# A recurrence among fill products: scores moved to chunks 0 and 1, more products a group, DVE's order written by hand

## The chip, the cores and the metric

One core of one Trainium2 chip runs the whole program. The metric is device microseconds for one execution. Engines are named as in the profile: PE (TensorE matmul), PEld (its weight loads), DVE (VectorE), ACT (ScalarE), POOL (GpSimd), SP (SyncE, which issues the DMAs here).

## The reference, cut to what matters

Two layers over 272 tokens (16 meta tokens and 256 real ones) of width 2048, all in float32: an RWKV-7 time mix, a squared-ReLU MLP, a gated linear attention, a second MLP, and a last norm. Only the time mix is touched by the change. Its core is a scan over tokens, for each of 32 heads of width 64:

```python
def step(S, inp):
    r_t, w_t, k_t, v_t, a_t, b_t = inp
    sa = einsum('bhvk,bhk->bhv', S, a_t)
    S = S * w_t[:, :, None, :] + sa[..., None] * b_t[:, :, None, :] + v_t[..., None] * k_t[:, :, None, :]
    y = einsum('bhvk,bhk->bhv', S, r_t)
    return S, y
```

Ahead of it stand the projections r, k and v and the low-rank decay and rate; behind it a per-head norm, a bonus term, a gate, and the output matrix `w_o`.

## The kernel before, in words

**Products.** Float32 matrices are multiplied in three passes. A weight piece of 128 x 1024 is loaded (`wload`, L122), ACT rounds it to `hi` (L132), DVE forms `lo = raw - hi` (L133), each in two halves in this stage, and PE adds hi·xh, hi·xl and lo·xh (`mm3`, L136; profile lines L138 to L140). One such triple of matmuls of 272 columns is called a *product* here; a piece holds eight. There are three `raw` buffers and two of `hi` and `lo`.

**The recurrence in chunks.** The scan is done in chunks of 64 tokens: four full ones and one of 16. Heads are taken in four groups g of eight. Within a chunk the scan is a triangular system. `scores` (L403) forms its matrices, eight matmuls a chunk, masked by two DVE operations. `invert` (L419) inverts all triangular blocks of a group at once on DVE: ten transposes into `sysA`, thirty elimination steps (each an `upd` product and a subtraction from `sysA`, the second needing the first), twelve transposes back. It is a generator with 52 steps, so that it can be spread over other work. `merge` (L518) joins 32 x 32 blocks to 64 x 64 on PE in two halves (profile lines L530 and L540), with ACT copies between.

**A chunk's chain.** `state` (L579) multiplies the state S into the chunk's rows and DVE forms `rs`; `solve` (L593) applies the inverse; `emit` (L604) makes the new S on PE (L611), which DVE adds and scales (two operations), and the outputs (L619); `inner` (L569) prepares the next chunk's `rs`. `turn` (L624) transposes outputs back to `hres`; `centre` (L548) and `keys` (L561) prepare values and keys. `norm(g)` (L635) is a generator of eight steps for the group's head norm and gate, with PE matmuls L643 and L652.

**Fill.** PE is kept busy beside this chain by 448 products: the v projection (256), `outA` (128) and half of `outB` (64). `R(n)` runs the next n of them and `until(n)` runs up to the n-th. The v projection of a column ends with an ACT copy and a DVE add to `rr`.

**What sets the order.** PE's order in this stage is the program's (`manual_schedule`, L745). All other engines, DVE among them, are ordered by the compiler's scheduler from priorities. `wload` has a high priority. The table `GAPS` (L46) gives for each group and chunk how many products stand between `state` and `solve`, and between `solve` and `emit`. After the last chunk `until(V - 8)` runs 120, 184 or 248 products in all, the rest of the inversion is issued, and `merge` follows. In group g, the scores of the next group are placed in chunks 0, 1 and 2, and `invert` starts in chunk 2, with 6 and 8 steps ahead of `solve` and of `emit`.

**The key stage ahead.** For each of 16 columns f: two weight pieces of `w_k`, exponentials on ACT, some sixteen DVE operations, and stores of `bk` and `ar` to DRAM, from which `load` (L398) brings a group back. Inversion 0 is issued whole at f = 13, its scores at f = 9.

Of the kernel before, what the change touches and what calls it, by code (L numbers as in the profile page):

```python
# [17 lines left out]
P = 128  # L18
# [9 lines left out]
NG = 4  # L28
# [14 lines left out]

GAPS = [[(2, 1), (2, 1), (2, 1), (8, 8), (8, 8)],  # L46
# [3 lines left out]


class Kern:
# [211 lines left out]
    def rwkv(self, done):  # L264
# [133 lines left out]
        def load(g, bk=True, ar=True):  # L398
            for on, dst, src in ((bk, BKs, bkd), (ar, ARs, ard)):
                if on:  # L400
                    nc.sync.dma_start(dst[g % 2], src[4 * g : 4 * g + 4].rearrange("f p n -> p f n"))

        def scores(g, c):  # L403
            BK, AR, AM, AMr = (b[g % 2] for b in (BKs, ARs, AMs, AMrs))
# [43 lines left out]
        for f in range(KT):  # L448
            r = rr[f]
            bk, ar = st2[0][f % 2], st2[1][f % 2]  # L450
            ps = self.proj(pair(wk, f), xk, T, bank=self.ptr if f % 2 else None)
            ca = self.t(ep, [P, 2, T], "ca", 2)
            nc.sync.dma_start(ca.rearrange("p a t -> p (a t)"), cad[f])
            iW, kk, sq, kn = (self.t(ep, [P, T], n, 2) for n in ("iW", "kk", "sq", "kn"))
            nc.scalar.activation(W, ca[:, 0], AF.Exp, scale=-DECAY)
            nc.scalar.activation(iW, ca[:, 0], AF.Exp, scale=DECAY)
            nc.scalar.mul(kk, ps, self.vec("k_k", f))
            nc.scalar.activation(sq, kk, AF.Square)
            nc.scalar.activation(kn, ca[:, 1], AF.Identity, scale=self.vec("k_a", f), bias=self.omka[:, f : f + 1])
# [12 lines left out]
            nc.vector.scalar_tensor_tensor(out=kn, in0=r, scalar=self.vec("r_k", f), in1=kn, op0=ALU.mult, op1=ALU.mult)  # L472
            put(ar, 1, r, W)
            nc.sync.dma_start(ard[f], ar)
            rk = self.pm()[:, :T]
            nc.tensor.matmul(rk, self.bones, kn, start=True, stop=True)
            nc.scalar.copy(r, rk)
            nc.vector.tensor_copy(WC[:, f], W[:, C - 1 : 4 * C : C])
            if f == 3:
                xv = mix(3, self.xp)  # L480
                early2.close()
                wl = ExitStack()
                lp = wl.enter_context(tc.tile_pool(name="wl", bufs=1, reuse_waits="tile"))
                BKs, ARs = ([self.t(lp, [P, 4, 576], n)] for n in ("BK0", "AR0"))
                AMs, AMrs = [self.t(lp, [P, NC4, 8, 128], "AM0")], [self.t(lp, [64, 8, 64], "AMr0")]
                sysA = self.t(lp, [P, 32, 32], "sysA")
                t11 = sysA.rearrange("p a b -> p (a b)")[64:96].rearrange("p (c h s) -> p c h s", c=NC4, h=8)
                nc.gpsimd.memset(sysA, 0.0)
            if f == 7:
                load(0)  # L490
            if f == 9:
                for c in range(5):
                    scores(0, c)
            if f == 13:
                for _ in invert(0):
                    pass
        early.close()

        win = ExitStack()
# [165 lines left out]
        loc = [hres[:, f] if f < 12 else rr[f - 4] for f in range(KT)]  # L665


        def units(x, srcs, ps):
            for i, s in enumerate(srcs):
                hi, lo = self.wload(s)  # L670
                for j in range(8):
                    kt = 8 * i + j
                    self.mm3(ps, hi, lo, slice(j * P, (j + 1) * P), x[kt][:, 0], x[kt][:, 1], kt == 0,
                             kt == 8 * len(srcs) - 1)
                    if kt < 8 * len(srcs) - 1:
                        yield

        def v_proj(f):
            ps = self.pj()[:, :T]
            yield from units(xv, pair(wv, f), ps)  # L680
            nc.scalar.copy(hres[:, f], ps)
            tt(rr[f], rr[f], hres[:, f])
            yield

        def outA(f):
            ps = self.pj()[:, :T]
            yield from units(yo, [ap["rw_oA"][f]], ps)
            xin = rr[f % 8] if f < 12 else loc[f]
            nc.sync.dma_start(xin, ap["hT"][:, f])
            tt(loc[f], ps, xin, ALU.add)  # L690
            yield

        def outB(s, fp):
            hi, lo = self.wload(ap["rw_oB"][s, fp])
            pss = [self.pj()[:, :T] for _ in range(2)]
            for i in range(2):
                for j in range(4):
                    y = yo[8 + 4 * s + j]
                    self.mm3(pss[i], hi, lo, slice((4 * i + j) * P, (4 * i + j + 1) * P), y[:, 0], y[:, 1], j == 0, j == 3)
                    if j < 3:  # L700
                        yield
                f = 2 * fp + i
                tt(hres[:, f] if s else loc[f], pss[i], loc[f], ALU.add)
                if s:
                    done(f)
                yield

        def products():
            for f in range(KT):
                yield from v_proj(f)  # L710
            split(0)
            split(1)
            for f in range(8):
                yield from outA(f)
            split(2)
            for f in range(2):
                yield from outB(0, f)
            for f in range(8, 12):
                yield from outA(f)
            for f in range(2, 6):  # L720
                yield from outB(0, f)
            for f in range(12, 16):
                yield from outA(f)
            for f in range(6, 8):
                yield from outB(0, f)

        work = products()
        ran = [0]
# [13 lines left out]
        nothing = iter(())  # L742
        self.split_parts = 2
        load(1)
        with tc.manual_schedule(engines={mybir.EngineType.PE}):  # L745
            until(52)
            m = merge(0)
            next(m)
# [4 lines left out]
                f(0, 0)  # L753
            inv = last = nothing
            for g in range(NG):
                V = 64 * (g + 2) if g < 3 else 0
                for c in range(5):
                    if c:
                        state(g, c)
                        turn(g, c - 1)  # L760
                    if g + 1 < NG and c in (1, 2):
                        scores(g + 1, 2 * c - 1)
                        R(1)
                    else:
                        some(last, 1)
                        R(GAPS[g][c][0])
                    some(inv, 6)
                    solve(g, c)
# [12 lines left out]
                    if c < 4:  # L781
                        inner(g, c + 1)
                    if c == 2 and g + 2 < NG:
                        load(g + 2, ar=False)
                some(last, 99)
                if g + 2 < NG:
                    load(g + 2, bk=False)
                if g + 1 < NG:
                    until(V - 8)
                    some(inv, 99)  # L790
                    m = merge(g + 1)
                    next(m)
                    until(V)
                    turn(g, 4)
                    R(4)
                    next(m)
                    for f in (centre, keys, inner):
                        f(g + 1, 0)
                    R(3)
                else:  # L800
                    turn(g, 4)
                last = norm(g)
        for _ in last:
            R(4)
        R(999)
        win.close()
        wl.close()
        split(3)
        for f in range(8):
            for _ in outB(1, f):  # L810
                pass
        self.split_parts = 1
        outer.close()

# [249 lines left out]
```

## Time and profile before

| what | us |
|---|---|
| median of 3 runs | 2668.19 (2666.27 to 2672.52) |
| the profiled execution | 2671.53 |
| its span | 2669.7 |
| PE, DVE, ACT busy | 2553.1, 1687.8, 1258.0 |
| PE waiting for an inversion's end, 318 to 700 us | 47.9 |

The first 300 us or so are the projections r and k; the recurrence lies between about 320 and 680; the rest are `outB`, the MLPs and the attention. A busy PE in this profile is not PE at its peak: matmuls are pipelined, so that a product is priced by the time from start to start. PEclk is the clock that the throttle granted, 1.00 at best.

### The profile page before, as it was taken

The page shows a single profiled execution, that of the slowest core. Times are in us where ns is not written, and L with a number is a line of the kernel's source. Part 1 is how long each engine was busy: PE and PEld are TensorE (multiplying, and loading weights), DVE is VectorE, ACT ScalarE, POOL GpSimd, SP SyncE. Part 2 cuts the span into 40 slices and gives each one's busy share as a digit, 9 for nine tenths or more (in the row PEclk, how much of TensorE's full clock was granted, in tenths as well). Part 3 has the DMA queues.
Part 4 walks back from the last instruction along what each step waited for, and adds up shares of the span by engine and source line. Part 5 has one row for each costly group of instructions (what it writes and reads, how often), then busy time and mean ns, then how long its engine had stood idle before and what let it go on. Part 6 is the DMA issues. An engine that isn't in the chain of part 4 may idle for free.

```text
span 2669.7 us, 47686 instructions
## 1 busy us (share of the span) xinstructions
PE 2553.1 (96%) x19492; PEld 2369.1 (89%) x19492; DVE 1687.8 (63%) x2794; ACT 1258.0 (47%) x2011; POOL 10.8 (0%) x35
## 2 busy tenths in 40 slices
PE   7999887779999999999999999999999999999998
PEld 7888886668999999999999999988888888888887
DVE  8678966674755545545545666776766656656665
ACT  5465543435554434434434544454555535435444
POOL 0000000000000000000000000000000000000000
PEclk9999988889999999999999999999999999999999
DMA  5567622213445555545555544444555555555554
GB/s 189 177 226 260 223 92 72 85 58 106 160 166 177 179 174 175 179 176 174 176 179 174 178 152 144 174 150 142 190 184 188 189 190 189 188 187 188 188 189 158
DMA packets 136026, 450.16 MB, mean 169 GB/s; under 512 B 14704, under 2 KB 22640, under 8 KB 135808
## 3 DMA queue, kind: packets, MB, share of 16 engines
q1 hardware_dynamic: 135808, 447.12, 48.4%
q8 instruction: 153, 2.51, 0.4%
q14 instruction: 65, 0.53, 0.1%
HBM read 431.07 MB, written 15.99 MB: 167 GB/s over the span
## 4 chain that ended last, share of the span: by engine, by line
PE 76%; DVE 1%; ACT 0%; issue 0%; DVEq 0%
PE pj L166 23%; PE pj L138 13%; PE pj L140 13%; PE pj L139 13%; PE pj L167 12%; PE pt L899 1%; DVE lo L133 0%; PE pu L908 0%; PE pm L652 0%; PE pt L888 0%; PE pu L910 0%; PE pu L909 0%; PE pm L845 0%; PE pm L643 0%; DVE hres L978 0%; DVE sg L927 0%
## 5 line engine op out<-in xcount | busy, mean ns | idle before, releaser
L133 DVE TENSOR_TENSOR lo<-raw,hi 128x1024 fp32r<-128x1024 f32 (+1 forms) x834 | 946.8, 1142 | 617.4 <-ACT hi L132 603.9
L132 ACT CAST hi<-raw 128x1024 fp32r<-128x1024 f32 (+1 forms) x834 | 813.4, 983 | 1098.5 <-PE pj L139 585.3
L138 PE MATMUL pj<-x,hi 128*128 128x272 f32 x2224 | 661.7, 298 | 6.6 <-ACT x L306 4.1
L140 PE MATMUL pj<-x,lo 128*128 128x272 f32 x2224 | 649.2, 292 | 0.0
L139 PE MATMUL pj<-x,hi 128*128 128x272 f32 x2224 | 647.3, 291 | 0.0
L166 PE MATMUL pj<-x,hi 128*128 128x512 f32 x1664 | 587.9, 397 | 0.6 <-DVE x L818 0.6
L167 PE MATMUL pj<-x,lo 128*128 128x256 f32 x1664 | 469.5, 282 | 1.3 <-DVE lo L133 1.3
L138 PEld LDWEIGHTS pj<-x,hi 128*128 128x128 f32 x2224 | 425.6, 191 | 15.3 <-ACT x L306 4.9
L139 PEld LDWEIGHTS pj<-x,hi 128*128 128x128 f32 x2224 | 428.1, 192 | 2.1
L140 PEld LDWEIGHTS pj<-x,lo 128*128 128x128 f32 x2224 | 424.9, 191 | 0.7
L166 PEld LDWEIGHTS pj<-x,hi 128*128 128x128 f32 x1664 | 313.5, 188 | 76.2 <-issue 2.9
L166 PE MATMUL pj<-h,hi 128*128 128x512 f32 x1024 | 358.5, 395 | 0.0
L167 PEld LDWEIGHTS pj<-x,lo 128*128 128x128 f32 x1664 | 315.0, 189 | 2.9 <-DVE lo L133 1.9
L138 PE MATMUL pj<-h,hi 128*128 128x272 f32 x1024 | 295.3, 288 | 0.0
L140 PE MATMUL pj<-h,lo 128*128 128x272 f32 x1024 | 294.4, 288 | 0.0
L139 PE MATMUL pj<-h,hi 128*128 128x272 f32 x1024 | 294.0, 287 | 0.0
L167 PE MATMUL pj<-h,lo 128*128 128x256 f32 x1024 | 288.9, 282 | 0.0
L166 PEld LDWEIGHTS pj<-h,hi 128*128 128x128 f32 x1024 | 192.7, 188 | 43.6
L167 PEld LDWEIGHTS pj<-h,lo 128*128 128x128 f32 x1024 | 194.3, 190 | 0.0
L139 PEld LDWEIGHTS pj<-h,hi 128*128 128x128 f32 x1024 | 194.1, 190 | 0.0
L138 PEld LDWEIGHTS pj<-h,hi 128*128 128x128 f32 x1024 | 193.2, 189 | 0.0
L140 PEld LDWEIGHTS pj<-h,lo 128*128 128x128 f32 x1024 | 192.4, 188 | 0.0
(246 smaller groups left out, 2213.9 us busy)
## 6 DMA issues: line engine op xcount, KB each, us to landing
raw<-mlp_w_d SPq DMA_DIRECT2D x512, 512.0 KB, 3.2
raw<-gla_in_d SPq DMA_DIRECT2D x98, 512.0 KB, 3.2
raw<-w_rkv_d SPq DMA_DIRECT2D x80, 512.0 KB, 3.4
raw<-gla_o_d SPq DMA_DIRECT2D x32, 512.0 KB, 3.2
raw<-w_r_d SPq DMA_DIRECT2D x16, 512.0 KB, 3.3
raw<-rw_oA_d SPq DMA_DIRECT2D x16, 512.0 KB, 3.2
raw<-rw_oB_d SPq DMA_DIRECT2D x16, 512.0 KB, 3.2
ard<-ar SPq DMA_DIRECT2D x16, 288.0 KB, 3.5
```

What stands on the lines that cost most here:

```text
L132: nc.scalar.copy(hi[:, h], raw[:, h])
L133: nc.vector.tensor_tensor(out=lo[:, h], in0=raw[:, h], in1=hi[:, h].bitcast(F32), op=ALU.subtract)
L138: nc.tensor.matmul(out, hi[:, ws], xh, start=first, stop=False)
L139: nc.tensor.matmul(out, hi[:, ws], xl, start=False, stop=False)
L140: nc.tensor.matmul(out, lo[:, ws], xh, start=False, stop=last)
L166: nc.tensor.matmul(wide, hi[:, ws], x[kt][:, :, off : off + SEQ], start=kt == 0, stop=False)
L167: nc.tensor.matmul(ps[:, :SEQ], lo[:, ws], x[kt][:, 0, off : off + SEQ], start=False, stop=kt == nk - 1)
L899: nc.tensor.matmul(pa[:w, i * C : (i + 1) * C], KX[i][:, dt, s * P : s * P + w], Q[:, dt, i * C : (i + 1) * C], start=dt == 0, stop=dt == 1)
```

## The change

It has five parts, all in the RWKV-7 function.

1. Scores of the next group go to chunks 0 and 1 alone (0 and 1 in chunk 0; 2, 3 and 4 in chunk 1). `invert` starts at the end of chunk 1, with nine steps ahead of each `solve` and each `emit`.
2. `GAPS` has 8 or 9 products twice in chunks 2 to 4 of groups 0 to 2, and 4 twice in all chunks of group 3. The merge comes after product 134, 214 or 286 (`MARK`); ahead of it in a group run 72 to 80 products from the last merge.
3. Inversion 0 is spread over the key products: seven steps a column from f = 8, after loads at f = 4 and scores at f = 6.
4. Weight pieces come from one list, and `ahead()` issues the load and the split of the next piece at the fourth product of the present one.
5. `manual_schedule` holds for DVE too, so its order there is the program's. The loads for group g + 2 are issued in chunks 2, 3 and 4, the second array cut at column 512.

```diff
-GAPS = [[(2, 1), (2, 1), (2, 1), (8, 8), (8, 8)],
-        [(2, 1), (2, 1), (2, 1), (8, 8), (8, 8)],
-        [(2, 1), (2, 1), (2, 2), (10, 10), (10, 10)],
-        [(2, 2), (2, 2), (10, 10), (10, 10), (10, 10)]]
+GAPS = [[(2, 1), (2, 1), (8, 8), (9, 9), (9, 9)],
+        [(2, 1), (2, 1), (8, 8), (9, 9), (9, 9)],
+        [(2, 1), (2, 1), (8, 8), (8, 8), (8, 8)],
+        [(4, 4), (4, 4), (4, 4), (4, 4), (4, 4)]]
+MARK = [134, 214, 286]
...
-            if f == 7:
+            if f == 4:
                 load(0)
-            if f == 9:
+            if f == 6:
                 for c in range(5):
                     scores(0, c)
-            if f == 13:
-                for _ in invert(0):
-                    pass
+                inv = invert(0)
+            if f > 7:
+                for _ in range(7):
+                    next(inv, None)
...
-        def units(x, srcs, ps):
-            for i, s in enumerate(srcs):
-                hi, lo = self.wload(s)
+        def units(x, n, ps):
+            for i in range(n):
+                hi, lo = weights.pop(0)
                 for j in range(8):
+                    if j == 3:
+                        ahead()
...
+        def ahead():
+            if srcs:
+                weights.append(self.wload(srcs.pop(0)))
...
+        ahead()
-        with tc.manual_schedule(engines={mybir.EngineType.PE}):
+        with tc.manual_schedule(engines={mybir.EngineType.PE, mybir.EngineType.DVE}):
...
-                    if g + 1 < NG and c in (1, 2):
-                        scores(g + 1, 2 * c - 1)
-                        R(1)
-                    else:
+                    if more and c < 2:
+                        scores(g + 1, 2 * c)
+                    elif not more:
                         some(last, 1)
-                        R(GAPS[g][c][0])
-                    some(inv, 6)
+                    R(GAPS[g][c][0])
+                    some(inv, 9)
                     solve(g, c)
...
-                    if g + 1 < NG and c < 3:
-                        scores(g + 1, 2 * c)
-                        if c == 2:
-                            inv = invert(g + 1)
-                    some(last, 3)
+                    if more and c < 2:
+                        scores(g + 1, 2 * c + 1)
+                    some(last, 4)
                     R(GAPS[g][c][1])
-                    some(inv, 8)
+                    if more and c == 1:
+                        scores(g + 1, 4)
+                        inv = invert(g + 1)
+                    some(inv, 9)
                     emit(g, c)
...
-                    until(V - 8)
+                    until(MARK[g])
                     some(inv, 99)
                     m = merge(g + 1)
                     next(m)
-                    until(V)
+                    R(4)
                     turn(g, 4)
-                    R(4)
+                    R(2)
                     next(m)
                     for f in (centre, keys, inner):
                         f(g + 1, 0)
-                    R(3)
+                    R(4)
```

The order of all other instructions in the stage, and what is computed, stay as they were.

More of the change, by code (lines that the diff above doesn't have):

```diff
@@ L396, in put, with fetch, load @@
             tt(dst[:, o + skip : o + 16], a[:, 4 * C + skip :], b[:, 4 * C + skip :])
[L398 to L401, printed above, removed]
+        def fetch(g, dst, src, a=0, b=576):
+            nc.sync.dma_start(dst[g % 2][:, :, a:b], src[4 * g : 4 * g + 4, :, a:b].rearrange("f p n -> p f n"))
+        def load(g):
+            fetch(g, BKs, bkd)
+            fetch(g, ARs, ard)
         def scores(g, c):
@@ L679, in v_proj @@
             ps = self.pj()[:, :T]
-            yield from units(xv, pair(wv, f), ps)
+            yield from units(xv, 2, ps)
             nc.scalar.copy(hres[:, f], ps)
@@ L686, in outA @@
             ps = self.pj()[:, :T]
-            yield from units(yo, [ap["rw_oA"][f]], ps)
+            yield from units(yo, 1, ps)
             xin = rr[f % 8] if f < 12 else loc[f]
@@ L697, in outB @@
                 for j in range(4):
+                    if (i, j) == (0, 3):
+                        ahead()
                     y = yo[8 + 4 * s + j]
@@ L706, in outB @@
                 yield
-        def products():
[L709 to L725, printed above, removed]
+        order = [(v_proj, f) for f in range(KT)] + [(split, 0), (split, 1)] + [(outA, f) for f in range(8)] + [(split, 2)]
+        order += [(outB, 0, 0), (outB, 0, 1)] + [(outA, f) for f in range(8, 12)] + [(outB, 0, f) for f in range(2, 6)]
+        order += [(outA, f) for f in range(12, 16)] + [(outB, 0, 6), (outB, 0, 7), (split, 3)]
+        order += [(outB, 1, f) for f in range(8)]
+        srcs = []
+        for k, *a in order:
+            srcs += pair(wv, a[0]) if k == v_proj else [ap["rw_oA"][a[0]]] if k == outA else [ap["rw_oB"][a[0], a[1]]] if k == outB else []
+        weights = []
+        def ahead():
+            if srcs:
+                weights.append(self.wload(srcs.pop(0)))
+        def products():
+            for k, *a in order:
+                if k == split:
+                    split(*a)
+                else:
+                    yield from k(*a)
         work = products()
@@ L744, in rwkv @@
         load(1)
-        with tc.manual_schedule(engines={mybir.EngineType.PE}):
+        ahead()
+        with tc.manual_schedule(engines={mybir.EngineType.PE, mybir.EngineType.DVE}):
             until(52)
@@ L755, in rwkv @@
             for g in range(NG):
-                V = 64 * (g + 2) if g < 3 else 0
+                more = g + 1 < NG
                 for c in range(5):
@@ L782, in rwkv @@
                         inner(g, c + 1)
[L783 to L788, printed above, removed]
-                    until(V - 8)
+                    if g + 2 < NG and c == 2:
+                        fetch(g + 2, BKs, bkd)
+                    if g + 2 < NG and c == 3:
+                        fetch(g + 2, ARs, ard, 0, 512)
+                    if g + 2 < NG and c == 4:
+                        fetch(g + 2, ARs, ard, 512)
+                if more:
+                    until(MARK[g])
                     some(inv, 99)
@@ L804, in rwkv @@
             R(4)
-        R(999)
+        until(448)
         win.close()
         wl.close()
[L808 to L811, printed above, removed]
+        R(999)
         self.split_parts = 1
```

7 lines of the change are left out of this document (3 added, 4 removed).

## The prediction

> **What bounds the kernel now.** I read the page first (span), then a table of busy time by stretches, cut at events of the recurrence, then the waits, then the order of time.
>
> ```profile
> span 2669.7 us, 47686 instructions
> ```
>
> ```profile
> 328.16:350.39 22.23, 20.50 (x286) 18.47 (x287) 5.50 (x10) 9.61 (x22) 0.94 (x1) 0.70 0.26 94
> 350.39:410.67 60.28, 44.98 (x670) 40.80 (x666) 51.01 (x121) 20.91 (x48) 0.68 (x2) 0.88 0.30 102
> 410.67:435.23 24.56, 22.28 (x322) 19.65 (x323) 8.28 (x16) 13.01 (x31) 0.94 (x1) 0.88 0.18 62
> 435.23:448.58 13.35, 11.21 (x176) 8.99 (x173) 6.38 (x13) 6.25 (x15) 0.52 (x1) 1.00 0.12 32
> 448.58:459.90 11.32, 8.37 (x158) 6.99 (x159) 9.26 (x19) 2.93 (x8) 0.00 (x0) 1.00 0.38 130
> 459.90:473.15 13.25, 12.30 (x168) 11.34 (x169) 12.35 (x34) 5.36 (x12) 0.16 (x1) 0.87 0.21 73
> 473.15:499.26 26.11, 12.76 (x158) 11.91 (x159) 24.71 (x61) 7.01 (x15) 0.00 (x0) 0.79 0.38 131
> 499.26:589.91 90.65, 66.97 (x976) 59.03 (x977) 63.22 (x149) 36.93 (x88) 1.62 (x3) 0.88 0.18 60
> 589.91:678.15 88.24, 83.53 (x1077) 75.77 (x1078) 43.52 (x88) 47.04 (x106) 0.52 (x1) 0.96 0.29 97
> 678.15:743.61 65.46, 62.97 (x490) 61.53 (x488) 51.74 (x105) 35.96 (x72) 0.00 (x0) 1.00 0.46 162
> ```
>
> Columns: stretch, length, busy PE, PEld, DVE, ACT, POOL, granted clock, DMA share, GB/s. The cuts are the first matmul of a merge (328.16, 410.67, 499.26, 589.91) or of a `state` (350.39, 435.23, 448.58, 459.90, 473.15); 678.15 is the last norm's end, 743.61 the MLP's first matmul. So a group takes 82.5, 88.6 and 90.7 us from merge to merge, and 88.2 in the last. Group 1 is seen in detail: up to 459.90 DVE has slack (23.9 of 49.2 us busy), behind it DVE is full (37.1 of 39.4) and PE is not.
>
> ```profile
> PE pt L530 <- DVE sysA L441: 47.9, 4, 14.9
> PE pu L587 <- DVE S L266: 12.9, 9, 3.2
> ```
>
> Between 318 and 700 us PE waits four times for the end of an inversion, 47.9 us, and nine times for the state S.
>
> ```profile
> 384.78 0.39 PE L138 MATMUL pj<-x,hi 128*128 128x272 f32 x1
> ...
> 388.00 0.29 PE L599 MATMUL pu<-rs,AMr 32*16 32x64 f32 x4
> ```
>
> Eight fill products (24 matmuls) run between these two starts: 3.22 us, **0.40 us a product**; durations of 0.29 overlap and can't be added.
>
> **The change part by part.** DVE's work is not cut, only placed. Group 1's:
>
> ```profile
> L133 DVE TENSOR_TENSOR lo<-raw,hi 128x512 fp32r<-128x512 f32 x16 | 10.3, 686 | 13.6 <-ACT hi L132 13.6
> L266 DVE TENSOR_TENSOR sysA<-sysA,upd 128x30 f32<-128x30 f32 (+14 forms) x30 | 9.9, 331 | 0.9
> L266 DVE TENSOR_TENSOR upd<-sysA 128x30 f32<-128x30 f32 (+14 forms) x30 | 9.9, 331 | 1.0
> ...
> L427 DVE STREAM_TRANSPOSE sysA<-AM 32x256 f32<-32x256 f32 x8 | 4.3, 581 | 0.1
> L590 DVE SCALAR_TENSOR_TENSOR rs<-pu,rs 64x256 f32<-64x256 f32 (+1 forms) x8 | 3.4, 421 | 2.4 <-PE pu L587 2.3
> ```
>
> ```profile
> 460.51 0.21 DVE L266 TENSOR_TENSOR upd<-sysA 128x30 f32<-128x30 f32 x1
> 460.75 0.21 DVE L266 TENSOR_TENSOR sysA<-sysA,upd 128x30 f32<-128x30 f32 x1
> ...
> 482.88 0.40 DVE L266 TENSOR_TENSOR sysA<-sysA,upd 128x240 f32<-128x240 f32 x1
> 483.31 0.41 DVE L266 TENSOR_TENSOR upd<-sysA 128x238 f32<-128x238 f32 x1
> ```
>
> An elimination pair costs 0.48 us (30 elements, 0.24 from start to start) to 0.87 (240, 0.43 each); the thirty pairs rise and fall between, 21.8 us in all: 5.0 for pairs 1 to 8, 7.7 for 9 to 17, 7.1 for 18 to 26, 2.1 for 27 to 30. A transpose takes about 0.55 in a run, a weight piece's split 1.2 (two halves of 0.69 that overlap).
>
> *Groups 0 to 2.* In the changed order nine transposes stand on DVE between the last scores and S of chunk 1, a transpose and pairs 1 to 17 between rs and S of chunk 2, pairs 18 to 30 and five transposes in chunk 3, the last seven transposes in chunk 4. DVE runs them in that order, so S waits behind the block, and behind S stand PE's next `state`, and rs, `solve` and all that follows.
> - Chunk 2: `state` and rs 1.7 (0.8 to the first, then two of 0.42), two splits 2.4, a transpose 0.6, pairs 5.0 and 7.7, an add of r 0.4, S 0.9: **18.8 us**. PE's own part of chunk 3 was 12.3 in the 459.90 stretch with 16 products, 10.6 without the halved clock (below); chunk 2 has no `centre`: 10.2. PE waits 8.6.
> - Chunk 3: 1.7 + 2.4 + 0.4 + 7.1 + 2.1 + 2.6 + 0.9 = **17.2**; PE with 18 products 11.4, so it waits 5.8.
> - Chunk 4: PE alone, 11.4 without `centre` (1.0) and S's and inner's matmuls (1.0): 9.4; then 12 products to the mark, 4.8. The inversion is done: no wait at the merge.
> - Chunk 1: 13.4 before (the 435.23 stretch), less 2.4 from emit to its end, plus 1.7 for a norm call more, 1.0 for a product and scores: PE is there after 13.7 (group 0, without norms, 8.2). Then DVE's two masks, nine transposes and S, 6.8 with the hand-overs, and in groups 1 and 2 the last norm's 0.4 ahead of the masks: **20.9** (15.0).
> The norms come from these rows: a `pm` bank that all of them share serializes them.
>
> ```profile
> 425.19 0.62 PE L643 MATMUL pm<-ysq,cst 128*128 128x272 f32 x2
> ...
> 428.78 1.18 PE L652 MATMUL pm<-gs,g 128*128 128x272 f32 x4
> 430.84 0.73 PE L643 MATMUL pm<-ysq,cst 128*128 128x272 f32 x2 [0.88 <-DVE hres L653]
> 432.14 1.19 PE L652 MATMUL pm<-gs,g 128*128 128x272 f32 x4 [0.58 <-ACT ysq L644]
> 432.96 0.49 PE L138 MATMUL pj<-x,hi 128*128 128x272 f32 x1
> ```
>
> Steps of 2.06, 1.30 and 0.82; four calls in one go (1.30, 2.06, 1.30, 0.82) are 5.5 us in chunk 0 and again in chunk 1. Chunk 0 was 10.0 (425.19 to 435.23); with a norm call at full price and scores moved in it is 12.1 (group 0, without norms: 6.5).
>
> ```profile
> 410.67:416.50 5.83, 5.83 (x81) 5.76 (x82) 0.92 (x2) 1.46 (x4) 0.94 (x1) 0.50 0.01 4
> ```
>
> The head from merge to chunk 0 was 14.5; less 2.9 for 5.8 us at half clock behind the merge and 1.2 for a split that PE no longer waits for, 10.4.
>
> The clock after a wait:
>
> ```profile
> 460.00:462.30 2.30, 2.30 (x53) 2.18 (x53) 2.00 (x8) 0.37 (x1) 0.16 (x1) 0.69 0.02 7
> 462.30:465.70 3.40, 3.40 (x22) 3.25 (x20) 3.20 (x9) 1.42 (x3) 0.00 (x0) 0.71 0.01 2
> ```
>
> Behind the 2.57 us wait before 459.90 the granted clock lacks 0.31 x 2.3 + 0.29 x 3.4 = 1.7 us of full speed. In chunks 2 and 3 such a loss lies inside PE's own wait; behind chunk 3's wait it doesn't: 2 us a group.
>
> The Trainium skill, "TensorE: Matmul & The Clock Gate", section "Part 1: The HAM clock gate", states that an idle window of about 3.4 us halves the clock and a busy one restores it. That speaks against this change, which trades one long wait a group for three of 5 to 9 us; by the page each would cost half a window, an estimate of 1.7 us, as the rows have it once. This is the ground of rival B.
>
> Sums: group 0 from `state` 1: 15.0 + 18.8 + 17.2 + 9.4 + 2 + 4.8 = 67.2 against 60.3, **+6.9** with 14 products more. Its head and chunk 0 (328.16 to 350.39): 22.2 at a granted clock of 0.70, 6.7 short of full speed, plus 1.0 for scores moved in: 16.5, **-5.7**. Group 1: 10.4 + 12.1 + 20.9 + 18.8 + 17.2 + 9.4 + 2 + 4.8 = 95.6 against 88.6, **+7.0** with 16 more. Group 2: the same with 3.3 for eight x splits in chunk 3, and 6 products fewer behind: 96.5 against 90.7, **+5.8**, 8 more.
>
> *Group 3 and the tail.* With 38 products already done, gaps of 4 replace those of 10: 33 products fewer, 13.1 us, since PE is the busy engine there (83.5 of 88.2); and the head's halved clock and late split, 4.6: **-17.7**. If the chain shows through the smaller gaps, up to 3 less. Five products fewer are left for the tail: **-2.0**.
>
> *The key stage.*
>
> ```profile
> 293.10:328.16 35.06, 25.97 (x197) 25.08 (x196) 34.44 (x97) 14.98 (x31) 0.00 (x0) 0.95 0.68 231
> ```
>
> ```profile
> 160.00:320.00 160.00, 155.22 (x1120) 145.75 (x1118) 145.01 (x379) 103.44 (x202) 2.06 (x3) 0.99 0.71 240
> ```
>
> ```profile
> 328.16 0.44 PE L530 MATMUL pt<-sysA,AM 32*32 32x32 f32 x9 [8.02 <-DVE sysA L441]
> ```
>
> DVE is full before the first merge; PE ended its 52 products 8.0 us ahead of it. Moving inversion 0 earlier leaves DVE's sum as it is, and DVE can gain only idle time (15 us in 160 to 320, 0.6 of it behind 293). In the changed order five splits stand behind inversion 0 and the last key block, so DVE gets there at about 320 (328.2, plus 1.1 for two transposes behind the wait's end, less 6.0 for the splits, less 1 for r adds, less 0 to 6 of idle time saved), needs 1.2 for the first split, and PE then has 28 products left, 11.2 us, after a wait that halves the clock: 333 instead of 328.2, **+5**. Ends: -3 (all idle time saved, clock up) and +10 (none saved).
>
> Total: 5 - 5.7 + 6.9 + 7.0 + 5.8 - 17.7 - 2.0 = **-0.7 us**. The profiled execution took 2671.5 (span 2669.7 and 1.8 around it), 3.3 above the median of 2668.2. I take the difference to the median: **2668 us**, no change. The waits for the inversion go, and as much comes back as waits for S.
>
> ```profile
> raw<-w_rkv_d SPq DMA_DIRECT2D x80, 512.0 KB, 3.4
> ```
>
> Edits at nothing: the loads cut at 512 and sent at chunks 2 to 4 (queued on SP between weight loads; DMA share 0.12 to 0.38 in group 1; if they block a weight load, one landing of 3.4 us). Splits a piece ahead: their gain is in the heads above.
>
> **Rivals.**
> A, faster: the blocks cost less than their sum, because DVE overlaps neighbours (the 0.69 halves do), chunk 4 keeps its clock, and the key stage saves its idle time. 6 for the clocks, 8 for the key stage: -14, 2654. For it: pairs beside foreign work cost some 0.08 less each. Against it: inside a block each pair depends on the last.
> B, slower: the clock halves after each of three waits a group and the loss isn't hidden, as PE's slow products push emit past DVE's arrival at S. That decides from a loss above the wait left, 5.8 in chunk 3. 1.7 us, nine times: +15, 2683. For it: the rows above; against it: PE's slack of 5 to 8 us.
> C: the edits don't do what they say, the merge still waits because splits fill DVE behind the transposes: 3 us a group, 2677.
>
> **How the numbers follow.** Forecast 0.50, A 0.20, B 0.25, C 0.05. The forecast's own range is 2658 to 2678 (key stage -8 to +5 around my value, 1.5 us on each DVE sum). Range with A and B: 2652 to 2686. A measurement tells 0.2%, 5.3 us, from no change. The forecast gives 0.13 faster, 0.24 same, 0.13 slower; A is faster; B slower; C 0.03 same, 0.02 slower: faster 0.33, same 0.27, slower 0.40.
>
> **What would show it.** Right: no wait of a merge matmul for `sysA`; S waits of 5 to 9 us in chunks 1 to 3 of groups 0 to 2; groups of about 96 us; the last norm's end near 679, with PE waiting for a split before the first merge at about 333. Wrong: S waits under 4 us (A), or a clock below 0.9 in chunk 4 and the heads (B).

## The result and the profile after

The changed kernel takes 2701.47 us (median of 4 runs, 2695.55 to 2704.59) against 2669.19 (median of 4, 2666.27 to 2672.52): ratio 1.0117, 95% interval 1.0101 to 1.0133. It is slower; the forecast was no change, and 2701 lies above its range. The profiled execution took 2695.55.

The page's span, then the table of stretches of the changed kernel, cut as in the prediction at the first matmul of a merge or of a `state`, at the last norm's end (704.91) and at the MLP's first matmul (768.12); columns: stretch, length, busy PE, PEld, DVE, ACT, POOL, granted clock, DMA share, GB/s.

```profile
span 2693.8 us, 47707 instructions
```

```profile
333.19:350.84 17.65, 15.93 (x302) 14.36 (x302) 6.98 (x12) 10.02 (x23) 0.95 (x1) 1.00 0.44 153
350.84:426.80 75.96, 54.33 (x696) 50.06 (x692) 52.16 (x123) 21.82 (x50) 0.68 (x2) 0.82 0.26 88
426.80:449.33 22.53, 19.59 (x324) 16.35 (x324) 9.19 (x17) 13.74 (x32) 0.95 (x1) 1.00 0.20 67
449.33:469.78 20.45, 13.38 (x199) 10.58 (x196) 13.84 (x27) 6.46 (x15) 0.52 (x1) 0.96 0.20 60
469.78:491.26 21.48, 12.64 (x164) 11.98 (x165) 16.70 (x44) 5.28 (x12) 0.17 (x1) 0.74 0.30 105
491.26:510.81 19.55, 13.47 (x175) 12.51 (x176) 15.21 (x40) 6.40 (x14) 0.00 (x0) 0.85 0.33 108
510.81:529.69 18.88, 16.75 (x170) 15.59 (x170) 9.32 (x18) 5.45 (x12) 0.00 (x0) 0.86 0.28 92
529.69:630.78 101.09, 74.40 (x1002) 65.48 (x1001) 67.54 (x155) 38.30 (x89) 1.63 (x3) 0.85 0.20 63
630.78:704.91 74.13, 69.05 (x981) 60.99 (x981) 38.16 (x78) 43.29 (x100) 0.52 (x1) 1.00 0.29 93
704.91:768.12 63.21, 60.72 (x472) 59.32 (x472) 50.18 (x103) 34.88 (x70) 0.00 (x0) 1.00 0.47 162
```

The MLP starts 24.5 us later than before (743.61), and the profiled executions differ by 24.0 (2671.53 before): all of these 24 us arise ahead of the MLP. The medians differ by 32.3, since the profiled execution after is the fastest of its four and the one before lies 2.3 above its median; for the other 8 us there is no profile. By stretches (us; the forecast column is the prediction's own sums):

| | before | forecast | after |
|---|---|---|---|
| first merge at | 328.2 | 333 | 333.2 |
| group 0 | 82.5 | 83.7 | 93.6 |
| group 1 | 88.6 | 95.6 | 102.9 |
| group 2 | 90.7 | 96.5 | 101.1 |
| group 3 | 88.2 | 70.5 | 74.1 |
| tail | 65.5 | 63.5 | 63.2 |

In group 1 the forecast had 22.5 up to `state` 1 (10.4 + 12.1) and 20.9 for chunk 1; the rows have 22.53 and 20.45. Chunks 2, 3 and 4 carry the miss: 21.5, 19.6 and 18.9 where it had 18.8, 17.2 and 16.2. PE's waits of the changed kernel from 318 to 790 us (engine, line and what it waited for; us in total, times, longest):

```profile
PE pu L592 <- DVE S L268: 56.1, 9, 9.1
PE pj L142 <- DVE lo L135: 6.7, 3, 2.5
```

No merge waits for the inversion (47.9 us in four before), but S is waited for 56.1 us in nine. What makes S late is read on DVE, in order of time, chunk 2 of group 1 (start, duration, instruction, and idle time ahead of it with its releaser):

```profile
471.04 0.88 DVE L595 SCALAR_TENSOR_TENSOR rs<-pu,rs 64x256 f32<-64x256 f32 x2 [1.40 <-PE pu L592]
473.89 1.29 DVE L135 TENSOR_TENSOR lo<-raw,hi 128x512 fp32r<-128x512 f32 x2 [1.98 <-ACT hi L134]
475.21 0.64 DVE L434 STREAM_TRANSPOSE sysA<-AMr 32x256 f32<-32x256 f32 x1
...
490.23 0.42 DVE L268 TENSOR_TENSOR S<-pu,S 128x256 f32<-128x256 f32 x1
```

and ACT's row of the cast that the split waits for:

```profile
473.24 1.14 ACT L134 CAST hi<-raw 128x512 fp32r<-128x512 f32 x2 [1.05 <-PE pj L141]
```

The cast needs a weight buffer that a fill product (L141) still reads, the split needs the cast, and in the fixed order the transpose and all elimination steps stand behind the split. DVE had ready steps behind the split and stood still. Its waits from `state` 2 to group 2's merge:

```profile
DVE r L268 <- ACT hres L687: 8.3, 2, 4.8
DVE lo L135 <- ACT hi L134: 4.0, 2, 2.0
DVE rs L595 <- PE pry L592: 2.7, 2, 1.4
DVE rs L595 <- PE pu L592: 1.4, 1, 1.4
```

These 16.4 us of 59.9 are what the experiments are about. (The stretch less DVE's busy time is 18.7 us; the other 2.3 are short gaps that the trace names no wait for.)

### The profile page after: what moved, and what is told of

It is laid out like the page before. It is cut to its first block, busy times and chain, and to the rows that moved or that the text cites. A ratio compares the mean times of both kernels' runs of the same rounds, so it can differ in the third digit from the quotient of the medians.

```text
span 2693.8 us, 47707 instructions
## 1 busy us (share of the span) xinstructions
PE 2563.6 (95%) x19492; PEld 2374.9 (88%) x19492; DVE 1688.3 (63%) x2794; ACT 1257.5 (47%) x2011; POOL 10.8 (0%) x35
## 4 chain that ended last, share of the span: by engine, by line
PE 88%; DVE 8%; ACT 2%; DMA 1%; issue 1%; SPq 0%; DVEq 0%; ACTq 0%
PE pj L168 23%; PE pj L140 14%; PE pj L141 14%; PE pj L142 14%; PE pj L169 12%; DVE lo L135 1%; DVE upd L268 1%; DVE sysA L268 1%; PE pj L195 1%; PE pt L416 1%; ACT hi L134 1%; PE pt L908 1%; PE pt L635 1%; DVE sysA L431 0%; PE pt L141 0%
## 5 line engine op out<-in xcount | busy, mean ns | idle before, releaser
L141 PE MATMUL pj<-x,hi 128*128 128x272 f32 x2224 | 649.1, 292 | 5.0 <-DVE x L268 5.0
L141 PEld LDWEIGHTS pj<-x,hi 128*128 128x128 f32 x2224 | 429.6, 193 | 7.3 <-DVE x L268 5.5
L141 PE MATMUL pj<-h,hi 128*128 128x272 f32 x1024 | 293.5, 287 | 0.0
L168 PEld LDWEIGHTS pj<-h,hi 128*128 128x128 f32 x1024 | 192.4, 188 | 44.5
L141 PEld LDWEIGHTS pj<-h,hi 128*128 128x128 f32 x1024 | 193.7, 189 | 0.0
```

Of the source, the lines that this page charges most:

```text
L141: nc.tensor.matmul(out, hi[:, ws], xl, start=False, stop=False)
L168: nc.tensor.matmul(wide, hi[:, ws], x[kt][:, :, off : off + SEQ], start=kt == 0, stop=False)
```

## The experiments

All ratios are to the kernel before, run on the same chip in the same rounds, with a 95% interval. Four theories: **1**, a split at the head of DVE's queue waits for its cast; **2**, the halved clock behind each wait; **3**, DVE's order by hand as such; **4**, formed later: the hand order costs the time for which DVE stands idle at its queue's head.

**a1_block_first**: the inversion's steps ahead of the fill products.

```diff
-                    R(GAPS[g][c][0])
-                    some(inv, 9)
+                    some(inv, 9)
+                    R(GAPS[g][c][0])
```

(The same with the second gap; in chunk 1 the last scores and the inversion's start move ahead with it.)

> The changed kernel with one move: in every half chunk the inversion steps are issued ahead of the fill products instead of behind them, so that on DVE they stand ahead of the weight split. Theory 1 (in the fixed DVE order the inversion block stands behind a split, the split behind ACT's cast, the cast behind a fill product; DVE stands still 2.0 us for it in chunk 2 and in chunk 3, and all behind it is late): these two stalls go, the waits for S shrink from 8.8 and 6.1 us in group 1 to about 7 and 4, 4 us a group, 12 in all: about 2690. Theory 2 (the halved clock behind each wait is the root: the products themselves are slow, and the block length alone sets the rest): the stall only moves, PE waits for the split instead, 0 to -3: about 2699 to 2702.

2680.73 us, ratio 1.0038 (1.0024 to 1.0052), against the 2690 that theory 1 gave. It is theory 1's sign and more than its size: chunks 2, 3 and 4 of group 1 last 19.4, 17.8 and 16.4 us, which is 2.1, 1.8 and 2.5 less. DVE's waits in the same stretch of this kernel (467.64 to 521.24):

```profile
DVE r L268 <- ACT hres L687: 4.5, 2, 3.3
DVE rs L595 <- PE pu L592: 2.8, 2, 1.4
DVE rs L595 <- PE pry L592: 1.3, 1, 1.3
DVE lo L135 <- ACT hi L134: 1.3, 1, 1.3
```

The wait for the cast fell from 4.0 to 1.3 and that for r (an add at a product's end, with the last transposes behind it) from 8.3 to 4.5. The order of two lines was worth 21 us.

**a2_warm**: PE is kept busy in its waits with added matmuls that nothing reads.

```diff
+        def warm(n):
+            d = self.pry()
+            for _ in range(n):
+                nc.tensor.matmul(d[:, :256], self.ident, self.cst[:, 128:384], start=True, stop=True)
...
+                        if more:
+                            warm([0, 0, 13, 20, 13][c])
                         state(g, c)
```

> The changed kernel with PE kept busy in its waits for S: 13, 20 and 13 matmuls of the identity with constants, 128x256, into a bank that nothing reads, ahead of the state products of chunks 2, 3 and 4 of groups 0 to 2. They add work and change no output. At an estimated 0.34 us each (half of a 128x272 f32 matmul pair's 0.72) they fill 4.4, 6.8 and 4.4 us of waits of 5.0, 8.8 and 6.1. Theory 2 (the halved clock is the root): the granted clock of chunks 2 to 4 rises from 0.60-0.68 behind the wait to 1.0, the cast comes 1.3 us earlier in chunks 2 and 3, chunk 4 loses 2.6 less: 5 us a group, about 2685. Theory 1 without the clock (the cast waits for a product whatever its speed): only chunk 4's 2.6 come back, about 2693. If an idle PE is not what lowers the clock: no change or slower by what the added matmuls overrun, 2701 to 2715.

2696.66 us, ratio 1.0097 (1.0069 to 1.0126). That is neither theory 2's 2685 nor a difference to the changed kernel (1.0101 to 1.0133) that can be told. The 6.7 to 7.1 us behind the three waits of group 1, first in the changed kernel, then here:

```profile
469.78:476.44 6.66, 6.66 (x72) 6.40 (x72) 3.20 (x7) 1.52 (x3) 0.17 (x1) 0.60 0.04 13
491.26:498.00 6.74, 6.74 (x79) 6.47 (x81) 3.37 (x8) 1.51 (x3) 0.00 (x0) 0.68 0.55 168
510.81:517.90 7.09, 7.09 (x77) 6.65 (x77) 2.13 (x4) 0.73 (x2) 0.00 (x0) 0.63 0.31 95
```

```profile
471.98:478.64 6.66, 6.66 (x103) 6.37 (x102) 4.36 (x12) 2.56 (x6) 0.16 (x1) 1.00 0.20 74
492.04:498.78 6.74, 6.74 (x102) 6.17 (x103) 4.70 (x11) 2.55 (x6) 0.00 (x0) 1.00 0.70 235
510.14:517.23 7.09, 7.09 (x105) 6.67 (x106) 3.33 (x7) 2.52 (x6) 0.00 (x0) 1.00 0.31 95
```

The third column from the right is the clock: 0.60, 0.68 and 0.63 became 1.00. Work for PE in its waits is all that was added, so the idle PE is what lowered it. The Trainium skill, "TensorE: Matmul & The Clock Gate", section "Part 1: The HAM clock gate", says that an idle window lowers the clock. The trace agrees: the changed kernel's three rows stand behind waits of 5.0, 8.8 and 6.1 us. In group 1 chunks 2 and 3 got 1.4 us shorter each and chunk 4 0.8, chunk 1 0.8 longer by the added matmuls, together 2.9 for the group. The clock is a small part, not the root.

**a3_dve_auto**: all of the change but DVE's order by hand.

```diff
-        with tc.manual_schedule(engines={mybir.EngineType.PE, mybir.EngineType.DVE}):
+        with tc.manual_schedule(engines={mybir.EngineType.PE}):
```

> The changed kernel with DVE's order left to the scheduler, PE's still by hand. Theory 3 (the hand order on DVE, nine inversion steps at a time ahead of S, is what costs; the rest of the change is worth what was forecast): the waits for S fall from 56 us in nine to some 13 in nine as before the change, the groups come to about 88 us, and the total to about 2670. Theories 1 and 2 (DVE has this work to do before the mark in any order; what was gained is lost to waits): S comes earlier, but the merges wait for the inversion again, 5 to 12 us each, and the total is 2690 to 2705.

2656.95 us, ratio 0.9946 (0.9928 to 0.9965): 44.5 us faster than the changed kernel, and faster than the kernel before. From `state` 2 to the next merge in group 1, first the changed kernel (its 469.78 to 529.69, as one stretch), then this one:

```profile
469.78:529.69 59.91, 42.85 (x508) 40.07 (x508) 41.23 (x102) 17.14 (x38) 0.17 (x1) 0.81 0.30 102
```

```profile
459.14:502.74 43.60, 37.49 (x508) 35.04 (x509) 41.07 (x102) 17.71 (x40) 0.16 (x1) 0.96 0.42 140
```

The same 508 matmuls and the same 41 us of DVE; only the length differs, by 16.3, and DVE's waits above were 16.4 us. With equal work that is bookkeeping; that the order makes the waits is shown by the edit, which changes nothing else. This kernel's DVE has one wait there:

```profile
DVE rs L595 <- PE pj L141: 0.2, 1, 0.2
```

How the scheduler does it, in order of time, around S of chunk 2:

```profile
470.56 0.38 DVE L268 TENSOR_TENSOR upd<-sysA 128x210 f32<-128x210 f32 x1
470.97 0.42 DVE L268 TENSOR_TENSOR S<-pu,S 128x256 f32<-128x256 f32 x1
471.31 0.37 DVE L268 TENSOR_TENSOR sysA<-sysA,upd 128x210 f32<-128x210 f32 x1
471.60 0.41 DVE L268 TENSOR_TENSOR S<-S,WC 128x256 f32<-128x256 f32 x1
```

S's two instructions lie between the product and the addition of one elimination pair, and while PE works from S to rs, steps go on. Theory 3 gave about 2670 and is the nearest, but the gain went past it: something else in the change is worth about 12 us, which the hand order hid.

**a4_key_old**: the changed kernel with the old key stage.

```diff
-            if f == 4:
+            if f == 7:
                 load(0)
-            if f == 6:
+            if f == 9:
...
-                inv = invert(0)
-            if f > 7:
-                for _ in range(7):
-                    next(inv, None)
+            if f == 13:
+                for _ in invert(0):
+                    pass
```

> The changed kernel with the key stage of the kernel before: load at f of 7, scores at 9, the whole inversion 0 at 13. If the early inversion itself cost the 5 us by which the first merge came later (PE stood for the scores at 218 to 240 us behind the load of group 0's keys, at a granted clock of 0.78), the first merge comes back to 328 us, the groups stay as they are, and the total falls by 5, to about 2696. If the splits a piece ahead or DVE's total work in the key stage set the 333 us, it stays at 333 or is later (a merge that waits for the inversion), and the total is 2700 or more.

2703.98 us, ratio 1.0110 (1.0080 to 1.0139), first merge at 334.5: no difference to the changed kernel (1.0101 to 1.0133) that can be told. The key stage is not the cause of the loss.

**b1_ahead, b2_recur, b3_auto_key**: the parts of the change, each with DVE's order by the scheduler (S and R are two theories that the first expectation states). b1 is the kernel before plus

```diff
-                hi, lo = self.wload(s)
+                hi, lo = weights.pop(0)
                 for j in range(8):
+                    if j == 3:
+                        ahead()
...
```

(with the list of pieces and the same in `outB`). b2 is a4_key_old with the scheduled DVE and `ahead()` right before each `weights.pop(0)`; b3 is a4_key_old with the scheduled DVE.

> The kernel before with one part of the change: weight pieces are loaded and split a piece ahead. DVE's order stays with the scheduler. Theory S (the gain of 12 us that the change shows with a scheduled DVE is that of the splits ahead): about 2657. Theory R (it is that of the recurrence's new order): 2665 to 2670, by the forecast's own price of 1.2 us a head, three or four heads, 4 us.

> The recurrence's new order alone (scores in chunks 0 and 1, gaps, marks, nine inversion steps, cut loads), with the old key stage, a split at its piece and a scheduled DVE. Theory R: about 2657, merges that wait for the inversion less than 6 us. Theory S: about 2669.

> All of the change but the DVE order by hand and the key stage. If the key stage's early inversion is worth what was hoped, this is slower than 2657, by up to the 8 us that the first merge waited before; if it costs (the scores of inversion 0 stop PE at 218 to 240 us, and the first merge came at 336.6), this is faster, to about 2650, with the first merge near 330. With the order by hand the old key stage changed nothing (2704 against 2701), which speaks for no change: 2657.

b1 2671.82, 0.9997 (0.9980 to 1.0014); b2 2657.87, 0.9939 (0.9916 to 0.9963); b3 2658.21, 0.9932 (0.9906 to 0.9959). So the splits ahead and the early inversion 0 are worth nothing that these runs can tell, and the recurrence's new order (scores, gaps, marks, blocks and loads together) is worth the 12 to 14 us: theory R.

**b4_before_hand**: the kernel before with DVE's order by hand, one line.

```diff
-        with tc.manual_schedule(engines={mybir.EngineType.PE}):
+        with tc.manual_schedule(engines={mybir.EngineType.PE, mybir.EngineType.DVE}):
```

> The kernel before with one part of the change: DVE's order in the recurrence by hand, which there is the order of the program. If the hand order costs by itself (S, rs and the splits stand behind blocks of inversion steps, whatever these blocks' sizes), about as much slower as it was in the changed kernel, 30 to 60: 2700 to 2730, with waits for S of 4 us and more. If it costs only with nine steps a block and the new marks, 2669 to 2680.

2740.56, 1.0256 (1.0216 to 1.0295): 68 us slower than the kernel before on the same chip (2672.31), more than the 30 to 60 expected. S is waited for 21.6 us in six here; most of PE's waits are at another place, since here a split stands at its piece:

```profile
PE pj L140 <- DVE lo L133: 56.9, 29, 5.9
```

PE waits for the split itself. In the changed kernel, whose splits stand a piece ahead, this wait is 6.7 us in three. That suggests a use of splits ahead under the hand order, but the two kernels differ in more than that, and no run took the splits ahead out of the changed kernel with its hand order.

**a6_hand6**: blocks of six steps in the hand order (`some(inv, 9)` to `some(inv, 6)`, twice).

> The changed kernel, DVE by hand as there, with six inversion steps a block instead of nine: a size. If S waits because of the length of the blocks that stand ahead of it, chunks 2 and 3 get shorter by some five and four steps of 0.8 us (21.5 to about 17.5, 19.5 to about 17), and what is left of the inversion fills the time in which DVE stood still in chunk 4, or is waited for at the merge by up to 5 us: 3 to 6 us a group, 2683 to 2692. If only the coarse order matters and not the size (any block ahead of S costs the same in the end, since DVE has the same work before the merge), no change: about 2700.

2699.38, 1.0106 (1.0085 to 1.0127): no change in the total, as the second theory had it. Its reason, that a block's size does not matter, is not what the profile shows. In group 1 chunk 2 fell from 21.5 to 15.7 us, and S is waited for less (35.7 us in 9). But the merges wait for the inversion again (7.7 in 3), and behind the first of these waits the clock was low up to `state` 1 (first row; the changed kernel's was 22.53 us at 1.00); the second row is `state` 2 to the merge (59.91 there):

```profile
430.38:458.07 27.69, 25.16 (x324) 21.36 (x325) 11.94 (x23) 13.84 (x32) 0.94 (x1) 0.75 0.17 52
476.89:533.19 56.30, 42.60 (x509) 39.70 (x509) 40.06 (x99) 17.13 (x38) 0.17 (x1) 0.85 0.33 109
```

So the group took 102.8 us (102.9 in the changed kernel). DVE's waits in the second row's stretch add to 13.9 us, against 16.4:

```profile
DVE r L268 <- ACT hres L687: 5.9, 3, 4.0
DVE lo L135 <- ACT hi L134: 3.9, 2, 2.0
DVE rs L595 <- PE pry L592: 2.7, 2, 1.4
DVE rs L595 <- PE pu L592: 1.4, 1, 1.4
```

The smaller block moves waits from S to the merge, and most of DVE's idle time stays. From here comes theory 4.

**a7_hand_fill**: the hand order, with steps put where DVE stands idle: eight ahead of the products as in a1, and two between S and the next rs.

```diff
...
                         inner(g, c + 1)
+                    if c:
+                        some(inv, 2)
```

> The changed kernel, DVE still by hand, with the inversion's steps put where DVE stands still: eight steps ahead of each half chunk's fill products instead of nine behind them, and two more between S and the next rs (the hand-over of 1.4 us from S over PE's state products to rs). Theory 4 (between state 2 and the merge DVE has 41 us of work in any order; the hand order costs exactly the time for which DVE stands at its head, 16.4 us in group 1 against 0.2 with the scheduler): DVE's idle time in group 1 falls from 16.4 us (12.3 with the block first alone) to some 7, the group to 92, and the total, over three groups, to about 2665. Theory 3b (it is the length of the blocks ahead of S, not DVE's idle time): as with the block first alone, 2681, or slower, since S is no earlier and rs is later by two steps, 1.6 us a chunk: 2681 to 2695.

2668.80, 0.9991 (0.9971 to 1.0011): 33 us faster than the changed kernel, in the hand order still, and within 4 of the 2665 expected. The stretch and DVE's waits in it:

```profile
462.69:512.64 49.95, 40.71 (x508) 37.94 (x508) 41.75 (x103) 17.13 (x38) 0.16 (x1) 0.86 0.36 122
```

```profile
DVE r L268 <- ACT hres L687: 4.4, 2, 3.3
DVE lo L135 <- ACT hi L134: 1.3, 1, 1.3
```

Group 1 takes 92.0 us (expected 92). DVE's idle time has to be taken by one measure: the stretch less its busy time is 18.7 us in the changed kernel, 12.3 in a1, 8.2 here (expected 7) and 2.5 in a3; the named waits are 16.4, 9.9, 5.7 and 0.2. (The expectation set the first kernel's 16.4 beside a1's 12.3, two measures.) The two steps make the sum smaller, as theory 4 says and 3b denies: the waits for rs are gone, and S is still waited for (5.8 at most).

**c1_inv_early, c2_mark, c3_early_mark, c4_early_mark, c5_norm, c6_early0_norm**: is DVE the bound then, and is there a better version? All on a3_dve_auto. c1 puts three scores into chunk 0, two at the head of chunk 1, and starts the inversion there; c2 has the last mark at 300; c3 has both. In c2 and c3 the split behind product 320 is issued ahead of the last norm calls of group 2, so the products behind it use values without those norms, and their times are bounds only; c4 is c3 with the mark at 298, where that split stands behind the norms.

```diff
-MARK = [134, 214, 286]
+MARK = [134, 214, 298]
...
-                        scores(g + 1, 2 * c)
+                        scores(g + 1, 3 * c)
+                        if c:
+                            scores(g + 1, 4)
+                            inv = invert(g + 1)
...
-                    if more and c < 2:
-                        scores(g + 1, 2 * c + 1)
+                    if more and c < 1:
+                        scores(g + 1, 1)
+                        scores(g + 1, 2)
...
-                    if more and c == 1:
-                        scores(g + 1, 4)
-                        inv = invert(g + 1)
```

c5 adds `R(1)` behind each of the norm's calls in chunks 0 and 1 of groups 1 and 2; c6 has all five scores and the inversion's start in chunk 0 besides.

> The changed kernel with a scheduled DVE, and the next group's inversion started half a chunk earlier: three of its scores in chunk 0, two at the head of chunk 1, inversion from there. If DVE's work before the merge bounds the groups once S is served in time (it stands idle in chunks 0 and 1 and is full from the inversion's start to the merge), the inversion ends some 3 to 5 us earlier a group, waits for S and the last merge's 5.6 us shrink: 2645 to 2652. If the groups are bound by PE's own order and the norms in chunks 0 and 1, no change: 2657.

> The changed kernel with a scheduled DVE and the last mark at 300 instead of 286: 14 products, 5.6 us, move from the tail ahead of the last merge, which waited 5.6 us for the inversion. If the wait is idle time that products can fill, about 2652; if their two splits (2.4 us of DVE) push the inversion's end on, the wait stays at 2 to 3 us and the total is about 2655.

> The two together. If the earlier inversion already takes the last merge's wait away, the 14 products only move, and this is as c1_inv_early, 2645 to 2652; if they add, 2640 to 2648.

> Scheduled DVE, inversion started half a chunk earlier, last mark at 298: with that the split that follows product 320 stands behind group 2's last norm. As c3_early_mark within noise, about 2645; if the 12 products that moved there gained only because that split ran too early, as c1_inv_early, 2649.

> The kernel of c4_early_mark with a fill product behind each of the norm's four calls in chunks 0 and 1 of groups 1 and 2. Each call leaves PE waiting 0.6 to 2.7 us (8.7, 5.9 and 2.5 us in all); a product of 0.40 us beside it is hidden. If PE's idle time there can be used: 8 products a group, 3.2 us less behind chunk 4, two groups: 2639. If DVE's work before the merge is the bound, the products that leave the stretch behind chunk 4 leave a wait for the inversion there: no change, 2645.

> The same with all five scores in chunk 0 and the inversion started behind them. If DVE's work before the merge bounds the groups, its idle time in chunks 0 and 1 is used and the merge comes some 3 to 6 us earlier in three groups: 2628 to 2636. If the scores' matmuls, which wait for two banks that DVE's masks set free, stand in PE's way in chunk 0: no better than c5_norm, or slower.

c1 2649.20, 0.9914 (0.9899 to 0.9929): as expected of a DVE bound, and no merge waits for the inversion. c2 2650.31, 0.9921 (0.9901 to 0.9940); c3 2644.82, 0.9912 (0.9881 to 0.9944). **c4 2646.20, 0.9906 (0.9869 to 0.9942)** is the best version found, though its interval overlaps c1's. c5 2651.51, 0.9933 (0.9913 to 0.9953): no gain. The profiles of c4 and c5 show where it went: groups 1 and 2 together took 174.3 us against 176.0 in c4, so 1.7 of the 6.4 us hoped for did come. But in c5 PE waited 3.2 us for `hres` just ahead of the last merge (1.5 in c4, 7 us ahead), and behind it the stretch up to `state` 1 of group 3 took 27.1 us at a granted clock of 0.76, against 22.5 at 1.00.

c6 2660.50, 0.9953 (0.9936 to 0.9971): no better than c5, as the second theory had it, though not by its reason alone. PE's scores wait for the masks 8.5 us in ten against 4.5 in nine in c4, but group 0 takes 33.3 us from its merge to `state` 1, against 21.7. The granted clock over these was 0.69 and 0.92: 0.31 x 33.3 less 0.08 x 21.7 is an estimate of 8.6 of the 11.7 us. From 343 to 361 us it was 0.50, with no wait of PE longer than 0.84 us in it or in the 10 us ahead; why, no run shows.

## Why the prediction was wrong

**Right.** The reading of what bounds the kernel; that the merge's waits go and come back as waits for S; the first merge at 333 (with the wait for the split, 2.5 us), though to the last us by luck, as the last section shows; chunks 0 and 1 of group 1; the tail; DVE's own durations: the elimination blocks of chunk 2 took 5.1 and 7.7 us (5.0 and 7.7 forecast). The splits ahead had 1.2 us a head in the forecast; b1, and b2 against b3, show no gain, and could not tell one so small. The last norm's end (679 forecast, 704.9 measured) missed with the groups.

**The step that failed** is "`state` and rs 1.7 ..., two splits 2.4, a transpose 0.6, pairs 5.0 and 7.7, ...: 18.8 us" for chunk 2, its like for chunk 3, and "PE alone, ...: 9.4; then 12 products to the mark, 4.8" for chunk 4. They add DVE's durations (chunk 2's terms as written add to 18.7) and put at nothing the time, but for the 0.8 us to the first rs, for which DVE stands at the head of its fixed order with ready work behind it. It had 16.4 us of waits in group 1's stretch. Of chunk 2's 2.7 us too much, the split's wait for its cast is 2.0, and 0.4 is the slower way from `state` to rs (2.1 with the clock at 0.60); chunk 3 the same; in chunk 4 the add of r held up the transposes and these the split, for which PE waits:

```profile
523.72 0.39 PE L142 MATMUL pj<-x,lo 128*128 128x272 f32 x1 [2.13 <-DVE lo L135]
```

Group 0 missed in the same places, with the same two waits for the cast (2.0 each) and the same wait of PE for the split (2.1). In group 2, chunks 2 and 3 have the waits for the cast too, PE also waits 4.4 us for the x splits, and chunk 4 missed by only 0.5. The groups' misses of 9.9, 7.3 and 4.6 are 21.8 of the 25 us by which the profile lies above the sum; group 3 gives 3.6, of which 3 had been allowed for "if the chain shows through the smaller gaps". The prediction asked what stands behind S and rs on DVE, but not what the instructions ahead of S wait for themselves: the splits stood in the sum as DVE's 1.2 us each. The sign stood in the prediction's own row of the splits in group 1 before: 13.6 us of idle time ahead of them, ended by ACT's cast.

**The rivals.** A was wrong by its ground: the blocks did not get cheaper by overlap (5.1 and 7.7 us); what makes room is that independent work fills the hand-overs, and that needs the other order. B had the sign and not the mechanism, so that "slower" had the largest chance (0.40) would have been luck. The clock did fall behind each wait (0.60 to 0.68 over some 7 us), but S was still waited for 5.7 and 6.1 us ahead of chunk 4 in groups 0 and 1 and 3.3 in group 2, so emit never came after DVE; the slow products delayed the cast instead. Kept at full clock, the kernel's median was 4.8 us lower, within the noise, not 15. C did not occur. The mechanism of the result, a fixed order that lets an engine stand, was no rival at all, though DVE's order by hand was a named part of the change. Priced alone it costs 44.5 us (a3); the rest of the change gains 12.

Where the gain of the new order likely comes from: the next group's inversion starts earlier, so that in a3 the merges ahead of groups 1 and 2 do not wait for it (11.6 and 13.4 us before). c1, which starts it earlier still and gains 8 us on a3, speaks for that; no run moves the inversion's start alone in the kernel before. Whether DVE's work bounds the best version stays open.

## What to carry to other kernels

An order written by hand costs on an engine whatever its queue's head waits for, while ready work stands behind: sum the waits of each instruction that you put ahead, not only the durations. Compare an engine's busy time in the same stretch under both orders: if it is equal and the length is not, suspect the order, and undo it to see. Before a part of a change is judged, undo the riskiest line alone: here one line hid a gain of 12 us behind a loss of 44.

## What was not expected

The same key stage brought the first merge at 333.2, 337.4, 337.8, 337.9 and 340.5 us in the changed kernel, a1, a2, a7 and a6: a single profile says where that merge comes to some 7 us only. And the cast's dependence on PE couples the two engines' speeds: with PE at full clock (a2), DVE's waits for the cast in the stretch fell from 4.0 to 2.0 us with nothing changed on ACT or DVE. A short wait of PE just ahead of a merge can also cost more behind it than it lasts: 2.1 us in a6 and 3.2 us in c5 stood ahead of stretches that were 5.2 and 4.6 us longer at a granted clock of 0.75 and 0.76. It need not: the same 2.1 us one group later in a6 was followed by 24.4 us at 0.93.
